# Scaling softmax rows in place and turning them with TensorE transposes, instead of matmuls with a diagonal of 1/sum

## The chip, the cores and the metric

The kernel runs on one core of a Trainium2 chip. The metric is the device time of one execution in microseconds (us), the median of several runs; lower is better. A core has a matrix engine (TensorE, PE in the profile, with its weight loads listed apart as PEld), a vector engine (VectorE, DVE), an activation engine (ScalarE, ACT), a general engine (GpSimd, POOL) and a queue engine that issues DMAs (SyncE, SP). Each engine works through its own queue in order. Matmuls write to PSUM, and only DVE and ACT read from there.

## The reference

Four transformer layers on 256 tokens of 1024 channels: neighbourhood attention with a context stream of another 256 tokens, sliding-window attention, a state space layer, and stick-breaking attention, each with a gated or squared-relu MLP. The change is in the softmax of the first two:

```python
s = jnp.concatenate([s_loc.reshape(B, H, GRID_W, n_loc), s_ctx], axis=-1)
p = jax.nn.softmax(s, axis=-1).astype(v.dtype)
p_loc = p[..., :n_loc].reshape(B, H, GRID_W, kh, kw)
p_ctx = p[..., n_loc:]
return (jnp.einsum('bhqkw,bkqwhd->bqhd', p_loc, v_win)
        + jnp.einsum('bhqc,bchd->bqhd', p_ctx, vc))
```

## The kernel before

Everything is float32. Products with weights are exact in three matmuls: weights and activations are split into a high and a low part (`split`, L228: ACT copies the high part, DVE subtracts), and `mm_w` and `mm_x` (L290 to L304) issue high by high, high by low and low by high. Weights come in by DMA parts of 512 KB or less as `raw`, and are split as `whi` and `wlo`.

The two attention stages work by chains. A chain is one head and one tile of 128 queries. In layer 0 there are 64: for each of 8 pairs of heads four chains over 512 keys (256 tokens and 256 of the context) and four context chains over 256 keys. In layer 1 there are 32, all over 512 keys. A chain runs through three functions:

- `score` (L1071, L1319): matmuls of q with k into a PSUM bank `sc`, a DVE addition of bias or mask, and `softmax_rows` (L818): DVE takes the row maximum (L821), ACT writes the exponentials to the tile `p` and their sum to `st` (L825), DVE takes the reciprocal of the sum (L829).
- `transposed` (L836): blocks of 128 columns of `p` are turned, so that keys lie on partitions, into a PSUM bank `pt`; then ACT and DVE, in turns, copy the bank to the SBUF tile `pT` (L843, L845).
- `finish` (L1087, L1330): for every second chain, matmuls of v with the two `pT` tiles into `po`, then a split to `oT`.

The turn and the scaling by 1/sum are one step before: `softmax_rows` makes `dg`, a diagonal matrix of 128 x 128 with each row's 1/sum (L831, `ts`, L122), and `transposed` multiplies each block by it:

```python
dg = at.tile([128, 128], F32, tag="dg", name="dg")
ts(dg, idn, st[:, 2:3], MUL)
T.matmul(pt[:, k * 128:(k + 1) * 128], lhsT=p[:, k * 128:(k + 1) * 128], rhs=dg)
```

In layer 0 the queries of the latent chains stand in reverse order within each row of 64 (the tile `q` is written reversed at L1017, since a bias table is read so), and `idn` is the constant `flip`, which turns them back; elsewhere it is the identity.

`run_chains` (L848) writes the chains in a staggered order: chain j is turned two chains (layer 1: three) after it was scored. Between chains stand pieces of other work (`fill`): the q and k products of the next pair of heads and their norms, in layer 1 the q products of the next group and the first part of the output product (`Early`, L319). The order in which instructions finally stand on each engine's queue is made by a scheduler from this program, with costs of its own for each instruction.

Of the kernel before, what the change touches and what calls it, by code (L numbers as in the profile page):

```python
# [24 lines left out]
def _layout():  # L25
    off = 0
    for name, n in (("id", 128), ("flip", 128), ("ones", 128), ("nam", 64), ("rc", 128),
                    ("rs", 128), ("sw0", 128), ("sw1", 128), ("hq", 2), ("dm", 16), ("eps", 1),
                    ("sel", 512)):
        _CL[name] = (off, off + n)  # L30
        off += n
    return off
# [5 lines left out]
def constants():  # L38
    c = np.zeros((128, _NC), np.float32)

    def put(name, a):
        s, e = _CL[name]
        c[:, s:e] = a

    p = np.arange(128)
    z = np.zeros((128, 128), np.float32)
    z[p, p] = 1.0
    put("id", z)
    f = np.zeros((128, 128), np.float32)
    f[p, (p // 64) * 64 + 63 - p % 64] = 1.0  # L50
    put("flip", f)
    put("ones", 1.0)
    col = 63 - p % 64
    start = np.clip(col - 8, 0, 48)
    kc = np.arange(64)
    ok = (kc[None] >= start[:, None]) & (kc[None] < start[:, None] + 16)
    put("nam", np.where(ok, 0.0, NEG).astype(np.float32))
    t = np.arange(256)
    inv = np.float32(10000.0) ** (-np.arange(16, dtype=np.float32) / np.float32(16))
    row = (t // 64).astype(np.float32)  # L60
    cl = (t % 64).astype(np.float32)
    ang = np.stack([row[:, None] * inv, cl[:, None] * inv], axis=1).astype(np.float32)
    cs, sn = np.cos(ang), np.sin(ang)
    cc = np.stack([cs, cs], axis=2).reshape(2, 128, 64)
    ss = np.stack([-sn, sn], axis=2).reshape(2, 128, 64)
    put("rc", cc.transpose(1, 0, 2).reshape(128, 128))
    put("rs", ss.transpose(1, 0, 2).reshape(128, 128))
    q, k = np.meshgrid(p, p, indexing="ij")
    put("sw0", np.where(k > q, NEG, 0.0))
    put("sw1", np.where(q > k, NEG, 0.0))  # L70
    put("hq", np.stack([np.where(p < 64, 0.125, 0.0), np.where(p < 64, 0.0, 0.125)], 1))
    put("dm", (p[:, None] % 16 == np.arange(16)[None]).astype(np.float32))
    put("eps", EPS)
    sel = np.zeros((128, 4, 128), np.float32)
    for q in range(4):
        sel[32 * q, q] = 1.0
    put("sel", sel.reshape(128, 512))
    return c
# [7 lines left out]
def _build(ctx, tc, I, out, dbg):  # L86
# [10 lines left out]
    last = [None]  # L97
# [51 lines left out]
    ident, flip, ones, eps = C("id"), C("flip"), C("ones"), C("eps")  # L149
# [22 lines left out]
    def vector_loads(va, cc):  # L172
        """loads of the small vectors, most urgent first."""
# [70 lines left out]
    class Weights:  # L244
        """src: dram view [128, kt, n] or [128, kt, n / 128, 128]; parts of at most 1024 elements."""
# [39 lines left out]
    def wpairs(w, s, c0):  # L285
        """two column tiles of 128, one in each of two neighbouring blocks of s columns."""
        b = w.rearrange("(k p) (b n) -> p k b n", p=128, n=s)
        return b[:, :, c0 // s:c0 // s + 2, c0 % s:c0 % s + 128]

    def mm_w(ps, w, c0, x, k, s0, s1, first, last_):  # L290
        """channel-major product, one contraction tile: weights stationary."""
# [6 lines left out]
    def mm_x(ps, w, c0, c1, x, k, t0, first, last_):  # L298
        """token-major product, one contraction tile: activations stationary."""
# [6 lines left out]
    def gemm_w(tiles, x, nk, s0, s1, evac, lead):  # L306
        """tiles: list of callables giving (weights, column, psum view, key); the first `lead` of them go
        through the contraction together, so that they can start before all of x is there."""
# [10 lines left out]
    class Early:  # L319
        """the first two column tiles of a product, begun while its last contraction tiles are still missing."""  # L320
# [78 lines left out]
    def square_sum(n, pooled, view=lambda v: v, late=KT - 2):  # L399
        """tiles whose columns sum, over the partitions, to those of h * h."""  # L400
# [20 lines left out]
    def rstd_rows(n, pooled=6, late=KT - 2):  # L421
        """1 / rms of every token, a quarter of them on each block of 32 partitions."""
# [19 lines left out]
    def rstd(n, pooled=6, late=KT - 2, tag="x"):  # L442
        """1 / rms of every token, on all partitions; left in PSUM."""
        return spread_cols(rstd_rows(n, pooled, late), n, tag)

    def rstd_cols(view=lambda v: v, pooled=6):
        """1 / rms of every token, tokens on partitions: [128, 2]; view gives the order of the tokens."""
# [11 lines left out]
    def gained(x, gain, view=lambda v: v):  # L459
        """x = gain * h, for products that are scaled by the tokens' 1 / rms afterwards."""  # L460
# [5 lines left out]
    def normed(x, r, n, gain, shift=None):  # L466
        """gain(k, v), shift(k, v): columns for contraction tile k and stream v."""
# [25 lines left out]
    def rsqrt(y, ss, n, pool):  # L493
        """y = 1 / sqrt(ss / 64 + eps), by a bit estimate and three Newton steps."""
# [10 lines left out]
    def head_scale(views, pool, scale=(None, None)):  # L505
        """1 / rms of every head of token-major products [128, 256] in PSUM, times a scale of the tokens."""
# [11 lines left out]
    def head_norm(views, pool, scale=(None, None)):  # L518
        """per-head normalisation of token-major products [128, 256]; views in PSUM."""
# [10 lines left out]
    def stack_q(o, q):  # L530
        """heads of q, token-major [128, n, 64], as blocks (high, low) of 128 columns."""
# [3 lines left out]
    def stack_k(oh, ol, k):  # L535
        """heads of k as blocks (high, high) and (low, low): with those of q, two products make the whole q k."""
# [12 lines left out]
    def cmul(o, a, b, t, conj=False, e=None):  # L549
        """o = a * b (pairs of real and imaginary views); conj: a * conj(b)."""  # L550
# [41 lines left out]
    class S5:  # L592
        """operators of the state space layer: e = a^s b, k = c a^t b, f = c a^t, and the phases of a^8t."""

        def __init__(self, pp, loads):
# [43 lines left out]
            # input matrix: ((a - 1) / lam) * b  # L639
# [32 lines left out]
        def c(self):  # L672
            pp, ct, ci, dr = self.pp, self.ct, self.ci, self.dr
            # output matrix, transposed: states onto partitions
# [101 lines left out]
        def phases(self, fp, hf):  # L776
            """powers 1..32 of exp(8 i theta), and |a|^8 with a zero where a new group starts."""
# [21 lines left out]
        def f(self, fp, i):  # L799
            """state-to-output matrices, a sixteenth of the groups: real(c a s) needs (re, -im) of c a."""  # L800
# [17 lines left out]
    def softmax_rows(ps, n, at, idn, tail=None):  # L818
        """rows of ps [128, n] -> unnormalised weights and idn scaled by the rows' 1/sum."""
# [10 lines left out]
        dg = at.tile([128, 128], F32, tag="dg", name="dg")  # L830
        ts(dg, idn, st[:, 2:3], MUL)  # L831
        return p, dg
# [3 lines left out]
    def transposed(p, dg, nk, at):  # L836
        pt = bank("pt")
        for k in range(nk):
            T.matmul(pt[:, k * 128:(k + 1) * 128], lhsT=p[:, k * 128:(k + 1) * 128], rhs=dg)
        pT = at.tile([128, 512], F32, tag="pT", name="pT", bufs=4)  # L840
        flip_evac[0] ^= 1
        if flip_evac[0]:
            act(pT[:, 0:nk * 128], pt[:, 0:nk * 128], AF.Copy)  # L843
        else:
            cp(pT[:, 0:nk * 128], pt[:, 0:nk * 128])  # L845
        return pT

    def run_chains(chains, lag):  # L848
        """chains: list of (score, probs, [finish of a group]); every group is two chains long.
        score() -> state, probs(state) -> transposed weights, finish([both])."""  # L850
# [13 lines left out]
    # ================ start ================  # L864
    w_pool("wsp", 4)
    with ExitStack() as sa:
# [92 lines left out]
        # ================ layer 0: mixer ================  # L959
# [4 lines left out]
        with ExitStack() as s0:  # L964
# [103 lines left out]
            def chain(pr, ctx_, qt, e, pre):  # L1068
                hd = 2 * pr + e

                def score():  # L1071
# [10 lines left out]
                    if ctx_:  # L1082
                        return softmax_rows(s_[:, 0:256], 256, at, ident)
                    tt(s_[:, 0:256], s_[:, 0:256], bts[hd, qt].rearrange("p r c -> p (r c)"), ADD)
                    return softmax_rows(s_, 512, at, flip)
# [15 lines left out]
                return (pre, score, lambda s_: transposed(*s_, 2 if ctx_ else 4, at), finish)  # L1101
# [33 lines left out]
        # ================ generic channel-major products ================  # L1135
        def w_tiles(src, ncols, ksteps=KT, r0=0, after=None):
            """column tiles of 128 of dram weights, loaded by chunks of at most 2048 elements."""
# [38 lines left out]
        with ExitStack() as s0:  # L1176
# [25 lines left out]
            # ================ layer 1: mixer ================  # L1202
# [4 lines left out]
        with ExitStack() as s0:  # L1207
# [4 lines left out]
            def rope(q, t, g):  # L1212
                """gain, then rotation of [128, 4 heads, 64] of tokens of tile t (None: gain alone)."""
# [58 lines left out]
            def q_steps(c, tag="g"):  # L1272
                """heads (8b + 2i, +1) of kv head 2b and the same four further on, of kv head 2b + 1"""
# [40 lines left out]
            def chain(c, s, qt, j, pre):  # L1314
# [4 lines left out]
                def score():  # L1319
# [8 lines left out]
                    return softmax_rows(s_, 512, at, ident, tail=sink[:, hd:hd + 1])  # L1328
# [12 lines left out]
                return (pre, score, lambda s_: transposed(*s_, 4, at), finish)  # L1341
# [41 lines left out]
    # ================ layer 1: the rest ================  # L1383
# [14 lines left out]
    def pair_products(src, n2, cols, x_, evac, lead, after=None):  # L1398
        """products with column tiles m and n2 + m of the weights, side by side."""
# [20 lines left out]
    # ================ S5 mixer ================  # L1420
    gT = [[actp.tile([128, 512], F32R, tag=f"o{p}{k}", name=f"g{p}{k}") for k in range(4)] for p in "hl"]
    gT = [[t[:, j * 256:(j + 1) * 256] for t in g_ for j in range(2)] for g_ in gT]
    with ExitStack() as s0:
# [4 lines left out]
        def spare_w():  # L1428
            """tiles of the pool of weight parts, which idles meanwhile."""
# [208 lines left out]
    # ================ stick-breaking attention ================  # L1638
# [146 lines left out]
    # ================ last gated mlp, and out ================  # L1785
# [44 lines left out]
```

## Time and profile before

| what | us |
|---|---|
| median of 3 runs | 1825.13 |
| lowest and highest run | 1824.33, 1829.41 |
| span of the profiled execution, first to last instruction | 1823.7 |
| PE busy in it | 1738.8 |
| DVE busy in it | 1183.4 |
| ACT busy in it | 790.0 |

The span leaves out what lies before the first and after the last instruction; of the profiled execution no other time is given, and its span is 1.4 us under the median of the runs. A PE busy time counts each matmul from its start to a modelled end; matmuls overlap in the array, so how long one holds the engine is read from starts that follow each other, not from its duration. A float32 matmul stands in the trace as two records, a float32 transpose as one.

### The profile page before, as it was taken

The page shows a single profiled execution, that of the slowest core. Times are in us where ns is not written, and L with a number is a line of the kernel's source. Part 1 is how long each engine was busy: PE and PEld are TensorE (multiplying, and loading weights), DVE is VectorE, ACT ScalarE, POOL GpSimd, SP SyncE. Part 2 cuts the span into 40 slices and gives each one's busy share as a digit, 9 for nine tenths or more (in the row PEclk, how much of TensorE's full clock was granted, in tenths as well). Part 3 has the DMA queues.
Part 4 walks back from the last instruction along what each step waited for, and adds up shares of the span by engine and source line. Part 5 has one row for each costly group of instructions (what it writes and reads, how often), then busy time and mean ns, then how long its engine had stood idle before and what let it go on. Part 6 is the DMA issues. An engine that isn't in the chain of part 4 may idle for free. (4 is left out here: it accounts for less than half of the span.)

```text
span 1823.7 us, 34377 instructions
## 1 busy us (share of the span) xinstructions
PE 1738.8 (95%) x13449; PEld 1537.9 (84%) x13449; DVE 1183.4 (65%) x2508; ACT 790.0 (43%) x1446; POOL 473.1 (26%) x633
## 2 busy tenths in 40 slices
PE   5899999999999999999999999998999999999999
PEld 3478888877777777888878999987899999889998
DVE  8556776775635434346986656768576788958674
ACT  4344444442413222223654545545444465535453
POOL 5311211115789300030102000202331332324130
PEclk8899999999999999999999999998999999999999
DMA  8565454325566655332215566688558564435852
GB/s 221 172 175 155 147 173 122 106 86 162 170 212 219 184 170 162 93 93 81 59 36 146 155 189 186 193 303 235 142 153 231 152 218 131 127 93 167 228 156 88
DMA packets 441045, 286.68 MB, mean 157 GB/s; under 512 B 50450, under 2 KB 418610, under 8 KB 440882
## 3 DMA queue, kind: packets, MB, share of 16 engines
q1 hardware_dynamic: 439122, 278.70, 52.4%
q0 software_dynamic: 1760, 5.77, 0.8%
q8 instruction: 106, 1.74, 0.4%
q14 instruction: 57, 0.47, 0.1%
HBM read 271.48 MB, written 17.15 MB: 158 GB/s over the span
## 5 line engine op out<-in xcount | busy, mean ns | idle before, releaser
L111 ACT ACTIVATE whi<-raw 128x1024 fp32r<-128x1024 f32 (+2 forms) x388 | 389.8, 1013 | 482.2 <-PE g L295 352.3
L114 DVE TENSOR_TENSOR wlo<-raw,whi 128x1024 fp32r<-128x1024 f32 (+2 forms) x388 | 466.4, 1207 | 189.8 <-ACT whi L111 186.7
L296 PE MATMUL g<-xh,wlo 128*128 128x256 f32 (+1 forms) x1216 | 375.2, 309 | 5.5 <-DVE wlo L114 5.2
L294 PE MATMUL g<-xh,whi 128*128 128x256 f32 (+1 forms) x1216 | 375.2, 310 | 1.3 <-ACT xh L111 1.2
L295 PE MATMUL g<-xl,whi 128*128 128x256 f32 (+1 forms) x1216 | 374.6, 308 | 0.0
L294 PE MATMUL g<-oh,whi 128*128 128x256 f32 (+1 forms) x1056 | 332.1, 315 | 3.3 <-DVE hc L117 1.4
L296 PE MATMUL g<-oh,wlo 128*128 128x256 f32 (+1 forms) x1056 | 331.0, 314 | 0.0
L295 PE MATMUL g<-ol,whi 128*128 128x256 f32 (+1 forms) x1056 | 330.8, 313 | 0.0
L296 PEld LDWEIGHTS g<-xh,wlo 128*128 128x128 f32 x1216 | 235.2, 193 | 17.9 <-DVE wlo L114 7.4
L294 PEld LDWEIGHTS g<-xh,whi 128*128 128x128 f32 x1216 | 234.7, 193 | 16.4 <-ACT whi L111 3.1
L295 PEld LDWEIGHTS g<-xl,whi 128*128 128x128 f32 x1216 | 235.3, 193 | 9.7
L294 PEld LDWEIGHTS g<-oh,whi 128*128 128x128 f32 x1056 | 198.3, 188 | 23.6 <-issue 3.9
L295 PEld LDWEIGHTS g<-ol,whi 128*128 128x128 f32 x1056 | 198.3, 188 | 15.3 <-issue 1.1
L296 PEld LDWEIGHTS g<-oh,wlo 128*128 128x128 f32 x1056 | 198.3, 188 | 14.5 <-issue 0.2
L302 PE MATMUL g<-whi,xh 128*128 128x256 f32 x560 | 166.9, 298 | 3.8 <-ACT xh L111 2.8
L303 PE MATMUL g<-wlo,xh 128*128 128x256 f32 x560 | 161.1, 288 | 0.6 <-DVE wlo L114 0.6
L304 PE MATMUL g<-whi,xl 128*128 128x256 f32 x560 | 160.5, 288 | 0.1
L117 DVE SCALAR_TENSOR_TENSOR h<-g,mods,h 128x256 f32<-128x256 f32 x64 | 30.8, 482 | 141.5 <-PE g L296 141.5
L302 PEld LDWEIGHTS g<-whi,xh 128*128 128x128 f32 x560 | 108.6, 194 | 13.3 <-issue 8.5
L303 PEld LDWEIGHTS g<-wlo,xh 128*128 128x128 f32 x560 | 108.8, 194 | 2.2 <-DVE wlo L114 1.7
L304 PEld LDWEIGHTS g<-whi,xl 128*128 128x128 f32 x560 | 108.1, 194 | 0.5 <-DVE xl L117 0.3
L111 ACT ACTIVATE oh<-t 128x256 fp32r<-128x256 f32 (+1 forms) x108 | 51.3, 482 | 125.5 <-DVE t L114 125.5
(300 smaller groups left out, 2943.3 us busy)
## 6 DMA issues: line engine op xcount, KB each, us to landing
raw<-mlp_w SPq DMA_DIRECT2D x128, 512.0 KB, 4.6
ada<-ada_w SPq DMA_DIRECT2D x88, 512.0 KB, 5.4
raw<-ffn_w_up SPq DMA_DIRECT2D x88, 512.0 KB, 5.2
raw<-ffn_w_down SPq DMA_DIRECT2D x32, 384.0 KB, 3.6
raw<-ffn_w_down SPq DMA_DIRECT2D x32, 320.0 KB
raw<-na_wqkv SPq DMA_DIRECT2D x32, 256.0 KB, 4.4
raw<-a_w_glu SPq DMA_DIRECT2D x16, 512.0 KB, 7.9
raw<-w_kv SPq DMA_DIRECT2D x16, 512.0 KB, 4.5
```

Of the source, the lines that this page charges most:

```text
L111: last[0] = A.activation(out=o, in_=i, func=f, **kw)
L114: (e or V).tensor_tensor(out=o, in0=a, in1=b, op=op)
L117: V.scalar_tensor_tensor(out=o, in0=a, scalar=s, in1=b, op0=op0, op1=op1)
L294: T.matmul(ps, lhsT=a, rhs=xh[k][:, s0:s1], start=first, stop=False)
L295: T.matmul(ps, lhsT=a, rhs=xl[k][:, s0:s1], start=False, stop=False)
L296: T.matmul(ps, lhsT=b, rhs=xh[k][:, s0:s1], start=False, stop=last_)
L302: T.matmul(ps, lhsT=xh[k][:, t0:t0 + 128], rhs=a, start=first, stop=False)
L303: T.matmul(ps, lhsT=xh[k][:, t0:t0 + 128], rhs=b, start=False, stop=False)
L304: T.matmul(ps, lhsT=xl[k][:, t0:t0 + 128], rhs=a, start=False, stop=last_)
```

## The change

`softmax_rows` no longer makes `dg`. It scales the whole tile `p` by 1/sum in place on DVE, 512 or 256 columns of 128 partitions. `transposed` turns the blocks with TensorE transposes, whose other operand is the constant identity. For the latent chains of layer 0 the queries are turned back by the copy from PSUM to `pT`, which reads each 64 columns in reverse. The constant `flip` is gone, so the tile of constants is 1363 columns wide instead of 1491. The other lines of the diff are comments taken out, so that line numbers from L17 to L830 stand 1 to 3 lower in the changed kernel; they are left out here.

```diff
-    def softmax_rows(ps, n, at, idn, tail=None):
+    def softmax_rows(ps, n, at, tail=None):
...
         V.reciprocal(out=st[:, 2:3], in_=st[:, 1:2])
-        dg = at.tile([128, 128], F32, tag="dg", name="dg")
-        ts(dg, idn, st[:, 2:3], MUL)
-        return p, dg
+        ts(p[:, 0:n], p[:, 0:n], st[:, 2:3], MUL)
+        return p
...
-    def transposed(p, dg, nk, at):
+    def transposed(p, nk, at, turned=False):
         pt = bank("pt")
         for k in range(nk):
-            T.matmul(pt[:, k * 128:(k + 1) * 128], lhsT=p[:, k * 128:(k + 1) * 128], rhs=dg)
+            T.transpose(pt[:, k * 128:(k + 1) * 128], p[:, k * 128:(k + 1) * 128], ident)
         pT = at.tile([128, 512], F32, tag="pT", name="pT", bufs=4)
+        o, i = pT[:, 0:nk * 128], pt[:, 0:nk * 128]
+        if turned:
+            o, i = o.rearrange("p (a x) -> p a x", x=64), i.rearrange("p (a x) -> p a x", x=64)[:, :, 63::-1]
         flip_evac[0] ^= 1
         if flip_evac[0]:
-            act(pT[:, 0:nk * 128], pt[:, 0:nk * 128], AF.Copy)
+            act(o, i, AF.Copy)
         else:
-            cp(pT[:, 0:nk * 128], pt[:, 0:nk * 128])
+            cp(o, i)
         return pT
...
-                        return softmax_rows(s_[:, 0:256], 256, at, ident)
+                        return softmax_rows(s_[:, 0:256], 256, at)
                     tt(s_[:, 0:256], s_[:, 0:256], bts[hd, qt].rearrange("p r c -> p (r c)"), ADD)
-                    return softmax_rows(s_, 512, at, flip)
+                    return softmax_rows(s_, 512, at)
...
-                return (pre, score, lambda s_: transposed(*s_, 2 if ctx_ else 4, at), finish)
+                return (pre, score, lambda s_: transposed(s_, 2 if ctx_ else 4, at, not ctx_), finish)
...
-                    return softmax_rows(s_, 512, at, ident, tail=sink[:, hd:hd + 1])
+                    return softmax_rows(s_, 512, at, tail=sink[:, hd:hd + 1])
...
-                return (pre, score, lambda s_: transposed(*s_, 4, at), finish)
+                return (pre, score, lambda s_: transposed(s_, 4, at), finish)
```

The number of instructions in the queues is the same on every engine. Their order differs in the two attention stages and nowhere else. Two places:

DVE in layer 0, around the second latent chain's scale. Ahead of it stand the norm of the next heads (`rq`, `ri`, `rt`, the steps of a reciprocal square root) and the third chain's bias, row maximum and copy. Before:

```order
L114 TENSOR_TENSOR sc<-sc,bt 128x256
L117 SCALAR_TENSOR_TENSOR rt<-rt,rq 128x8
L821 TENSOR_REDUCE st<-sc 128x1
L117 SCALAR_TENSOR_TENSOR ri<-rt,ri 128x8
L127 COPY pT<-pt 128x512
L114 TENSOR_TENSOR rt<-ri 128x8
L829 RECIPROCAL st<-st 128x1
L117 SCALAR_TENSOR_TENSOR rt<-rt,rq 128x8
L122 TENSOR_SCALAR dg<-cst,st 128x128
```

With the change:

```order
L124 COPY pT<-pt 128x512
L114 SCALAR_TENSOR_TENSOR rt<-rt,rq 128x8
L818 TENSOR_REDUCE st<-sc 128x1
L114 SCALAR_TENSOR_TENSOR ri<-rt,ri 128x8
L111 TENSOR_TENSOR rt<-ri 128x8
L114 SCALAR_TENSOR_TENSOR rt<-rt,rq 128x8
L114 SCALAR_TENSOR_TENSOR ri<-rt,ri 128x8
L111 TENSOR_TENSOR rt<-ri 128x8
L114 SCALAR_TENSOR_TENSOR rt<-rt,rq 128x8
L826 RECIPROCAL st<-st 128x1
L114 SCALAR_TENSOR_TENSOR ri<-rt,ri 128x8
L119 TENSOR_SCALAR p<-p,st 128x512
```

The copy of the turned block now stands ahead of the row maximum, and the reciprocal and the scale stand four small norm steps later.

PE in layer 1. Before, from the matmuls of v ahead of the 12th chain's turn: behind the turn come products with weights for the next group of q (`g<-whi,xh` and its two partners).

```order
L1324 MATMUL sc<-ka_8505,qz_9226 128x512
L1334 MATMUL po<-pT,vv 64x128 x7
L839 MATMUL pt<-dg,p 128x128 x4
L1324 MATMUL sc<-kb_8507,qz_9226 128x512
L1334 MATMUL po<-pT,vv 64x128
L303 MATMUL g<-wlo,xh_8350 128x256
L304 MATMUL g<-whi,xl_8358 128x256
L302 MATMUL g<-whi,xh_8351 128x256
L303 MATMUL g<-wlo,xh_8351 128x256
L304 MATMUL g<-whi,xl_8359 128x256
```

With the change, from the 16th chain's turn to the 18th's:

```order
L1334 MATMUL po<-pT,vv 64x128
L836 MATMUL pt<-cst,p 128x128 x4
L1324 MATMUL sc<-ka_8442,qz_9470 128x512
L1324 MATMUL sc<-kb_8444,qz_9470 128x512
L1334 MATMUL po<-pT,vv 64x128 x7
L1324 MATMUL sc<-ka_8442,qz_9477 128x512
L1324 MATMUL sc<-kb_8444,qz_9477 128x512
L836 MATMUL pt<-cst,p 128x128 x4
L1324 MATMUL sc<-ka_8442,qz_9477 128x512
L836 MATMUL pt<-cst,p 128x128 x4
L1324 MATMUL sc<-kb_8444,qz_9477 128x512
```

The products for q now all stand ahead of the 8th chain's turn, before the change ahead of the 13th's; from the 8th turn to the 20th PE has next to nothing but the chains.

## Rows read from the trace of the kernel before

**Rows 1.** The page: the span, and each engine's busy time and instructions.
```profile
span 1823.7 us, 34377 instructions
PE 1738.8 (95%) x13449; PEld 1537.9 (84%) x13449; DVE 1183.4 (65%) x2508; ACT 790.0 (43%) x1446; POOL 473.1 (26%) x633
```

**Rows 2.** Stretches of both chains: busy us of PE, PEld, DVE, ACT, POOL, clock.
```profile
132.00:406.00 274.00, 270.40 (x2370) 235.70 (x2370) 194.62 (x627) 121.38 (x308) 49.02 (x59) 0.99 0.45 132
880.00:985.00 105.00, 99.65 (x805) 84.25 (x805) 88.08 (x326) 57.32 (x148) 2.41 (x3) 0.98 0.15 44
```

**Rows 3.** Waits of PE on another engine, layer 0 chains, then layer 1 chains.
```profile
PE pt L839 <- DVE dg L122: 0.6, 1, 0.6
...
PE pt L1300 <- DVE pT L127: 2.5, 2, 1.6
```

**Rows 4.** Records of two lines of PE: durations in ns, minimum, median, maximum.
```profile
L839 PE MATMUL pt<-dg,p x640: 270/275/583, 132.7 to 978.3; 128*128 128x128 f32 x160
L1742 PE MATMUL pt<-cst,be x48: 271/273/329, 1526.2 to 1600.1; 128*128 128x128 f32 x48
```

**Rows 5.** Timeline of PE (start, us busy): diagonal matmuls, later float32 transposes.
```profile
303.28 1.16 PE L839 MATMUL pt<-dg,p 128*128 128x128 f32 x8
304.19 0.36 PE L302 MATMUL g<-whi,xh 128*128 128x256 f32 x1
...
1526.16 0.49 PE L1742 MATMUL pt<-cst,be 128*128 128x128 f32 x3
1526.49 0.72 PE L1675 MATMUL pt<-cst,qn 128*128 128x128 f32 x4
1526.97 0.36 PE L302 MATMUL g<-whi,xh 128*128 128x256 f32 x1
```

**Rows 6.** Groups of DVE by line and shape: count, busy us, mean ns.
```profile
L122 DVE TENSOR_SCALAR dg<-cst,st 128x128 f32<-128x128 f32 x96 | 27.4, 286 | 1.1
L114 DVE TENSOR_TENSOR h<-g,h 128x256 f32<-128x256 f32 x40 | 16.2, 420 | 19.3 <-PE g L296 19.3
L117 DVE SCALAR_TENSOR_TENSOR h<-g,mods,h 128x256 f32<-128x256 f32 x64 | 30.8, 482 | 141.5 <-PE g L296 141.5
L114 DVE TENSOR_TENSOR ol<-po,oh 128x512 fp32r<-128x512 f32 x8 | 5.5, 684 | 1.8 <-ACT oh L111 1.8
L122 DVE TENSOR_SCALAR qz<-pt,vt 128x512 f32<-128x512 f32 x4 | 3.0, 739 | 0.0
L127 DVE CAST q<-pt 128x512 fp32r<-128x512 f32 x8 | 5.4, 676 | 0.8 <-PE pt L1013 0.8
```

**Rows 7.** Layer 0 in 10 us windows: first and last of six, of 28.
```profile
152.00:162.00 10.00, 9.78 (x95) 8.36 (x91) 9.62 (x27) 6.07 (x14) 3.16 (x3) 1.00 0.66 181
372.00:382.00 10.00, 10.00 (x80) 8.67 (x79) 9.25 (x33) 5.03 (x14) 0.78 (x2) 1.00 0.63 182
```

**Rows 8.** Layer 1 in four windows, columns as in rows 2.
```profile
880.00:896.00 16.00, 16.00 (x127) 15.19 (x126) 15.68 (x55) 11.13 (x24) 0.00 (x0) 1.00 0.34 99
896.00:925.00 29.00, 29.00 (x239) 24.51 (x238) 24.90 (x102) 15.95 (x44) 0.00 (x0) 1.00 0.07 20
925.00:951.00 26.00, 22.28 (x191) 18.30 (x191) 24.00 (x97) 14.47 (x40) 0.00 (x0) 0.99 0.07 21
951.00:978.00 27.00, 27.00 (x215) 21.85 (x212) 19.42 (x69) 13.37 (x39) 0.00 (x0) 0.94 0.14 40
```

**Rows 9.** Windows around a fall of the granted clock, then of the last attention.
```profile
947.25:950.66 3.41, 1.80 (x18) 1.32 (x18) 3.41 (x13) 1.58 (x5) 0.00 (x0) 1.00 0.00 0
950.66:954.07 3.41, 3.41 (x18) 2.53 (x16) 2.65 (x6) 0.74 (x2) 0.00 (x0) 0.50 0.00 0
1584.00:1598.00 14.00, 12.14 (x76) 7.81 (x74) 13.77 (x22) 7.58 (x19) 11.33 (x34) 1.00 0.27 76
```

**Rows 10.** Transposes of PE within two of these windows, by line.
```profile
L1300 PE MATMUL pt<-idr,sq 128*128 128x128 f32 x8 | 1.2, 253 | 1.6 <-DVE pT L127 1.6
...
L1742 PE MATMUL pt<-cst,be 128*128 128x128 f32 x18 | 3.2, 285 | 1.3 <-DVE be L114 0.9 <-DVE pT L127 0.4
```

More of the change, by code (lines that the diff above doesn't have):

```diff
@@ L26, in _layout @@
     off = 0
-    for name, n in (("id", 128), ("flip", 128), ("ones", 128), ("nam", 64), ("rc", 128),
+    for name, n in (("id", 128), ("ones", 128), ("nam", 64), ("rc", 128),
                     ("rs", 128), ("sw0", 128), ("sw1", 128), ("hq", 2), ("dm", 16), ("eps", 1),
@@ L48, in constants @@
     put("id", z)
-    f = np.zeros((128, 128), np.float32)
-    f[p, (p // 64) * 64 + 63 - p % 64] = 1.0
-    put("flip", f)
     put("ones", 1.0)
@@ L147, in C @@
         return cst[:, s:e]
-    ident, flip, ones, eps = C("id"), C("flip"), C("ones"), C("eps")
+    ident, ones, eps = C("id"), C("ones"), C("eps")
     vt = const.tile([128, 384], F32, name="vt")
```

## Prediction

> **What bounds the kernel now.** I read the page first [rows 1]: PE is busy 95% of the span, DVE 65%. An average over a whole program says little about one stage, so next come the two stretches that the change touches [rows 2]. In layer 0 PE is busy 270.4 of 274 us and DVE 194.6 (71%); in layer 1 PE 99.7 of 105 and DVE 88.1 (84%). Then the waits of PE inside the chains [rows 3]: 0.6 us in all for the diagonal in layer 0, 2.5 us for copied blocks in layer 1. So PE hardly waits, and what is taken off its queue shortens a stage until DVE has no room left. How near that point is shows only in short windows. In layer 0, of 28 windows of 10 us from 132 us on, six have DVE busy for 9.0 us or more; the first and the last of them stand in [rows 7]. In layer 1 I cut at the changes of pattern [rows 8]: in 880 to 896 both engines are full (DVE 15.68 of 16), in 896 to 925 PE is full and DVE at 24.90 of 29, in 925 to 951 DVE (24.00 of 26) leaves PE idle for 3.7 us, and in 951 to 978 PE is full and DVE at 19.42 of 27.
>
> **PE: what is removed.** There are 64 chains in layer 0, half with four blocks and half with two, so 192 blocks, and 32 chains with four in layer 1, so 128: 320 in all. Before, a block is two records: 640 for 320 [rows 4]. A float32 transpose elsewhere in this kernel (L1742) is one: 48 records for 16 chains with three each. Durations (275 and 271 ns) say nothing, since records overlap; the starts do [rows 5]. Four blocks by the diagonal hold PE from 303.28 to 304.19, 0.91 us or 0.228 a block. Three transposes go from 1526.16 to 1526.49, four from 1526.49 to 1526.97: 0.11 to 0.12 each. I take 0.11 us saved per block: 21.1 us in layer 0, 14.1 in layer 1, 35.2 in all. The low end is 0; the trace excludes that transposes hold PE longer than now, at this clock.
>
> **DVE: what is added.** `dg` (128 columns) costs 0.286 us, 96 times [rows 6]. The scale has 512 columns in 64 chains and 256 in 32. No row has exactly this operation from SBUF in place. Two float32 tensors cost 420 ns at 256 columns and 684 at 512, so 1.03 ns a column; a scalar read per partition adds some 62 ns (482 against 420). An operation at that slope with 128 columns would take 420 - 132 + 62 = 350 ns, yet `dg` takes 286. So an operation on one SBUF tensor runs below that slope; near half of it (0.53 ns) is my reading. Then 512 columns cost 286 + 384 x 0.53 = 489 ns, and 256 cost 354. Bounds: no less than `dg` itself, 286; no more than the pointer scale from PSUM, 739 ns at 512 (`qz`), and 482 at 256. I take 489 and 354, since `dg` is the nearest row: the same operation, SBUF to SBUF, same operands. DVE gains 32 x 0.203 + 32 x 0.068 = 8.7 us in layer 0 and 32 x 0.203 = 6.5 in layer 1; at the high end 20.8 and 14.5.
>
> The Trainium skill's page "VectorE: DVE Perf Modes", section "The perf-mode tier table", says that a float32 tensor_scalar on SBUF goes at twice the pace of a tensor_tensor, and that an operand in PSUM takes this away. By its figure for 2,048 columns (1,227 ns), an estimate for 512 is some 0.43 us, and the whole sum below would come to about 1805. The trace agrees as far as `dg` reaches; no row has the wide scale.
>
> **Waits and moved steps.** The turn now waits for the scale instead of the diagonal, 0.2 us later after the same reciprocal, and in the order shown for DVE four small norm steps stand ahead of it as well. What is queued behind it on PE are the scores and v products of other chains. The cover is that a chain is turned two chains (layer 0, some 4.3 us each) or three (layer 1, some 3.1 us each) after its score, so some 8 to 9 us; that PE waited 0.6 us for `dg` in layer 0 [rows 3] says that the cover holds. I take nothing; if the cover were gone, the whole scale would be exposed (a rival below). The reversed read from PSUM: the reversed write of `q` from PSUM takes 676 ns at 512 columns, a forward addition 684 [rows 6], so nothing on DVE. For ACT no row shows it; ACT is busy 121 of 274 us in layer 0 [rows 2], and at twice the price of today for half of the 32 copies it would still have room. The scheduler moves 33 issues on SP and 6 on POOL within the two stages; weights for the next products are then asked for somewhat earlier or later, while the DMA share is 0.45 in layer 0 and 0.15 in layer 1, so nothing again. The constants are 64 KB smaller: nothing.
>
> **The sum.** Layer 0: in 22 of 28 windows PE sets the pace and its saving counts, 21.1 x 22/28 = -16.6. In the six where DVE is full the saving is lost and DVE's extra counts, 8.7 x 6/28 = +1.9. Together -14.7. Layer 1, by [rows 8]: 880 to 896, three chains on a full DVE, +0.6. In 896 to 925, nine chains, PE needs 29 - 36 x 0.11 = 25.0 and DVE 24.90 + 9 x 0.203 = 26.7; DVE is never packed perfectly, so I take some way between 26.7 and 29, -1.5. In 925 to 951, eight chains on DVE, +1.6. In 951 to 978, twelve chains, PE needs 21.7 and DVE 21.9: 5.1 to gain, taken as -4. Together -3.3. DVE is busy for 84.0 of these 98 us, so 90.4 with the scale: layer 1 cannot gain more than 7.6 us whatever PE saves. Total -18.0. The profiled span is 1823.7, 1.4 us under the median of the runs; I carry that over: 1825.1 - 18.0 = **1807 us**.
>
> **Rivals.** *Full saving.* The new order spreads DVE's work so that PE's 35.2 us count in full: 1790. For it: a scheduler may fill DVE's slack, 79 us in layer 0. Against it: the bound of 7.6 us in layer 1 allows only 21.1 + 7.6 = 28.7, or 1796; for the rest PE would have to save more per block than read.
>
> *The scale at its high price.* In place, with input and output the same tile, the scale might lose the fast pace and cost 0.74 us. Layer 0: -16.6 + 20.8 x 6/28 = -12.1. Layer 1: +1.4, 0 (DVE 29.0 of 29), +3.6 and some -1.5, so +3.5. Total -8.6: 1816.5. `dg` speaks against it, no row for a wide tile excludes it.
>
> *No change.* DVE's high price stands exposed on every chain, 35.3 us against 35.2 saved: 1825. This wants DVE to set the pace everywhere, which 79 us of slack in layer 0 speak against.
>
> *Slower: the clock.* PE gets half speed in some stretches. After 947.25 to 950.66, in which PE is busy for 1.80 of 3.41 us, the granted clock stands at 0.50 for the next 3.41 us, the lower of two levels (1.2 instead of 2.4 GHz) [rows 9]. Eight of the 18 matmuls ahead of that fall are transposes [rows 10]. If attention with transposes, and with more idle time of PE between them, drew this fall again and again, each such 3.41 us would cost up to 1.7. To be slower by over 5.5 us it must first eat the 18 gained: 23.5 / 1.7, or some 14 stretches of half clock. In all 28 that fit into the 95 us of layer 1 it would be +48, less 18: 1855. Against it: from 1584 to 1598 PE is busy 12.14 of 14 us with 18 transposes of L1742 among 76 matmuls, at a clock of 1.00 [rows 9, 10], and in 925 to 951 PE already idles 3.7 us and loses little of its clock. I take one such stretch more or less as inside the range.
>
> The Trainium skill's page "TensorE: Matmul & The Clock Gate", section "Part 4: PE-mode transpose", says that the full clock does not engage for transposes, as these do not count as PE work in the same way. By that rule alone the result would be this rival's 1855 at the most. The trace speaks against it where transposes stand among other matmuls, as they do here, and does not exclude it at 947 to 954.
>
> *It does not do what it says* (a float32 transpose as two passes, like the product): excluded by the 48 records of L1742 [rows 4].
>
> **How the numbers follow.** The forecast, 1798 to 1814 on its own, has 0.62; the full saving (1788 to 1797) 0.13; the high price (1814 to 1821) 0.12; no change 0.08; the clock 0.05. The range of 1789 to 1820 takes in the first three but for their edges and leaves out the last two. About 0.3%, 5.5 us, is what a measurement of this kernel can tell from no change. Faster by more than that, below 1819.7: the forecast and the full saving, and most of the high price, 0.85. Within 0.3%: no change and the edge of the high price, 0.10. Slower: 0.05.
>
> **What would show it.** In the profile of the changed kernel the turn must be 320 records with starts 0.11 to 0.12 us apart; 640 or 0.2 would take the forecast's ground away. The scale's group shows 0.49 or 0.74 us for 512 columns, and with it which case it is. The stage that was 132 to 406 us should end some 15 us earlier, the one from 880 on be some 3 us shorter, with DVE over 90% busy there and waits of PE for a scaled `p` or a copied `pT` where DVE is full. Layer 0 gaining far less than 15 us with DVE idle would mean that the cover of the turn is gone: then the transposes' group shows idle time ahead of it, put down to DVE's scale. A granted clock of 0.50 in several windows of layer 1 would show the last rival. A changed time in any stage outside these two would be nothing that I reasoned about.

## The result and the profile after

The changed kernel takes 1812.5 us (median of 4 runs, 1810.9 to 1814.1), the kernel before 1827.3 (4 runs, 1824.3 to 1829.7, one more than the forecast started from): a ratio of 0.991, 95% interval 0.990 to 0.993, so 14.8 us faster. The profiled execution has a span of 1809.2 us against 1823.7, 14.5 us less; all that follows is read from it. The page of the changed kernel, its span and engines [rows 1]:

```profile
span 1809.2 us, 33749 instructions
PE 1717.4 (95%) x13129; PEld 1504.4 (83%) x13129; DVE 1197.0 (66%) x2508; ACT 790.6 (44%) x1446; POOL 470.6 (26%) x633
```

PE has 320 matmul records fewer, DVE 13.6 us more work. To place the 14.5 us I cut both traces at the same instructions: layer 0 from the first turn of q (`turn`, L1013) to the last product with v, layer 1 from the first score to the last product with v. The columns are busy us (instructions) of PE, PEld, DVE, ACT, POOL, then the mean granted clock, the DMA share and GB/s. Before:

```profile
115.97:405.59 289.62, 282.70 (x2472) 246.73 (x2473) 200.98 (x644) 128.00 (x322) 52.72 (x64) 0.99 0.47 135
886.81:980.20 93.39, 89.25 (x722) 74.55 (x721) 77.92 (x305) 51.34 (x138) 0.00 (x0) 0.98 0.12 34
```

The changed kernel:

```profile
116.71:392.13 275.42, 269.57 (x2281) 226.06 (x2281) 207.07 (x644) 127.23 (x322) 54.48 (x64) 0.99 0.49 141
873.00:967.50 94.50, 81.82 (x594) 61.24 (x593) 83.12 (x305) 52.41 (x138) 0.00 (x0) 0.91 0.12 34
```

Layer 0 is 14.2 us shorter. Layer 1 is 1.1 us longer, although PE is busy for 7.4 us less there. What lies ahead of layer 0 (+0.7), between (-0.4) and behind (-1.7) is code that the change doesn't touch; in the kernels below those three parts move by up to three us too, once by 4.5, so a difference of that size in one profile means nothing there.

The scale as groups of DVE, over the whole span, then at 512 columns in layer 0 and in layer 1 alone:

```profile
L119 DVE TENSOR_SCALAR p<-p,st 128x512 f32<-128x512 f32 x64 | 32.2, 504 | 0.5
L119 DVE TENSOR_SCALAR p<-p,st 128x256 f32<-128x256 f32 x32 | 12.2, 383 | 0.3
...
L119 DVE TENSOR_SCALAR p<-p,st 128x512 f32<-128x512 f32 x32 | 16.9, 530 | 0.5
...
L119 DVE TENSOR_SCALAR p<-p,st 128x512 f32<-128x512 f32 x32 | 15.2, 478 | 0.0
```

The turn, as starts on PE (start, us busy; the first row of each pair is a turn, the second what follows it):

```profile
226.38 0.66 PE L836 MATMUL pt<-cst,p 128*128 128x128 f32 x4
226.79 0.36 PE L299 MATMUL g<-whi,xh 128*128 128x256 f32 x1
...
233.75 0.44 PE L836 MATMUL pt<-cst,p 128*128 128x128 f32 x2
233.94 0.36 PE L299 MATMUL g<-whi,xh 128*128 128x256 f32 x1
```

The scale costs 0.504 us at 512 columns in the mean (0.489 was forecast) and 0.383 at 256 (0.354). The means are drawn up by a few in layer 0: 61 of the 64 wide ones take 0.470 to 0.490 us, all of layer 1's among them, and the other three 0.98 to 1.02, each beside a running GpSimd instruction; at 256 columns most take 0.342 to 0.355 us, and the two longest, 0.82 and 0.91, also run beside GpSimd. In layer 1, where GpSimd is idle, the mean is 0.478. Four transposes hold PE for 0.41 us and two for 0.19, about 0.10 a block, where four products by the diagonal held it for 0.91 [rows 5]. That is 0.125 us saved a block; over all 192 blocks of layer 0, from the start of each turn to the start of what follows, 44.5 us became 22.7, or 0.114 a block. The forecast was 0.11.

In layer 1 the granted clock falls twice. For each fall, the 3.4 us ahead of it and the time at half clock:

```profile
907.30:910.72 3.42, 1.41 (x6) 0.59 (x4) 3.42 (x14) 1.15 (x5) 0.00 (x0) 1.00 0.00 0
910.72:920.96 10.24, 7.89 (x37) 5.84 (x38) 8.10 (x28) 4.99 (x14) 0.00 (x0) 0.50 0.00 1
931.30:934.70 3.40, 1.57 (x8) 0.69 (x5) 3.40 (x15) 1.72 (x6) 0.00 (x0) 0.99 0.00 0
934.70:941.53 6.83, 4.50 (x27) 3.71 (x28) 5.96 (x19) 2.67 (x7) 0.00 (x0) 0.51 0.00 0
```

Ahead of each fall DVE is busy without a gap and PE for less than half of the time. Then PE runs at 0.50, 17.1 us in all, or five stretches of 3.41 us; before it was one [rows 9]. What PE waits for, by the waits of that stage, is the next group's q, whose norm and rotation stand on DVE between the chains' steps (us in total, times, longest; before, the same wait was 0.6 us, once, beside the 2.5 of [rows 3], which are 0.9 now):

```profile
PE pt L1300 <- DVE sq L111: 5.4, 2, 2.7
```

### The profile page after: what moved, and what is told of

Same layout as the page of the kernel before. It is cut to its first block, busy times and chain, and to the rows that moved or that the text cites. A ratio compares the mean times of both kernels' runs of the same rounds, so it can differ in the third digit from the quotient of the medians.

```text
span 1809.2 us, 33749 instructions
## 1 busy us (share of the span) xinstructions
PE 1717.4 (95%) x13129; PEld 1504.4 (83%) x13129; DVE 1197.0 (66%) x2508; ACT 790.6 (44%) x1446; POOL 470.6 (26%) x633
## 5 line engine op out<-in xcount | busy, mean ns | idle before, releaser
L293 PEld LDWEIGHTS g<-oh,wlo 128*128 128x128 f32 x1056 | 198.4, 188 | 14.5 <-issue 0.3
```

The costliest lines, as they stand in the source:

```text
L293: T.matmul(ps, lhsT=b, rhs=xh[k][:, s0:s1], start=False, stop=last_)
```

## The experiments

Three theories for layer 1. **A**: DVE's time for the scale is what it pays. **B**: layer 1 gains, and something else falls short. **C**: the new order of the steps costs it. A fourth price, the half clock, is told apart on the way. Stages are cut as above, each in the one profiled execution of its kernel; the half clock is counted in layer 1, in stretches of 3.41 us, the length of the fall in [rows 9]. Each ratio is to runs of the kernel before taken beside that kernel (medians 1827.3 to 1829.7).

Two limits hold for all of it. The changed kernel and e1, e4, e6, e7, e8, e14 and e15 have the same layer 0 in the same order, and it took 274.4 to 276.2 us: a stage from one profile is good to about 1 us. And the scheduler orders the queues anew for each program. In layer 1 only before and e1, e4 and e11, and e6 and e9 share an order on PE and DVE, so every other comparison there changes the order along with the work.

| kernel | median, us | ratio to before | layer 0 | layer 1 | half clock |
|---|---|---|---|---|---|
| before | 1827.3 | | 289.6 | 93.4 | 1 |
| changed | 1812.5 | 0.990 to 0.993 | 275.4 | 94.5 | 5 |
| e1, layer 0 only | 1810.1 | 0.988 to 0.992 | 275.4 | 93.3 | 1 |
| e2, no scale | 1796.6 | 0.981 to 0.985 | 265.1 | 82.8 | 1 |
| e3, identity by matmul | 1839.4 | 1.004 to 1.008 | 291.2 | 100.1 | 2 |
| e4, layer 1 copies on ACT | 1807.2 | 0.987 to 0.990 | 276.2 | 88.6 | 4 |
| e6, layer 1 scale on GpSimd | 1815.3 | 0.990 to 0.995 | 275.4 | 95.3 | 1 |
| e7, filler | 1814.2 | 0.989 to 0.995 | 275.3 | 95.8 | 1 |
| e8, held order | 1820.5 | 0.994 to 0.997 | 275.1 | 103.2 | 7.7 |
| e9, both scales on GpSimd | 1823.8 | 0.995 to 0.998 | 280.9 | 99.3 | 4 |
| e11, all copies on ACT | 1800.1 | 0.982 to 0.987 | 269.3 | 87.6 | 3 |
| e14, lag of four | 1807.5 | 0.986 to 0.990 | 274.4 | 91.1 | 4 |
| e15, GpSimd and lag of four | 1810.6 | 0.988 to 0.992 | 275.9 | 93.0 | 4 |
| e16, e11 and lag of four | 1799.8 | 0.981 to 0.985 | 270.2 | 85.9 | 4 |

**One layer alone (e1).** Layer 1 keeps the diagonal:

```diff
+        if diag:
+            dg = at.tile([128, 128], F32, tag="dg", name="dg")
+            ts(dg, ident, st[:, 2:3], MUL)
+            return p, dg
```

> Layer 0 as changed, layer 1 as before (diagonal of 1/sum and matmuls). Theory A, DVE fills in layer 1 and PE, starved, falls to half clock, so the change gains nothing there: the time is that of the changed kernel, 1812 within 3 us, and the granted clock of 0.50 in the chains of layer 1 shrinks from five stretches of 3.41 us to one or two. Rival B, layer 1 does gain what its PE saving says and layer 0 falls short: 1815 to 1818, above the changed kernel.

1810.1 us, not to be told from the changed kernel by their intervals, and layer 1 back at 93.3 us with one stretch at half clock. The profiled execution was its slowest, 1814.8 us; what it has over the others is not in the two stages. The whole gain is layer 0's; B is out.

**One part of the change each (e2, e3).** e2 leaves out the scale, and with it the division by the row sums; e3 keeps it and turns by a product with the identity:

```diff
-        ts(p[:, 0:n], p[:, 0:n], st[:, 2:3], MUL)
```

> The changed kernel without the scale; the division by the row sums is left out. DVE is 64 x 0.48 + 32 x 0.35 = 42 us less busy than in the changed kernel, 27 less than before. Theory A, the work on DVE is what ate layer 1's gain: layer 1 falls 7 to 10 us below before, layer 0 some 19 to 21 below; in all 1796 to 1800, at full clock in layer 1 but for one stretch. Rival C, the order in which the steps now stand (the products for q all ahead of the chains) is what costs layer 1, and not the scale's work: layer 1 as in the changed kernel, 1808 to 1812, with the falls of the clock.

```diff
-            T.transpose(pt[:, k * 128:(k + 1) * 128], p[:, k * 128:(k + 1) * 128], ident)
+            T.matmul(pt[:, k * 128:(k + 1) * 128], lhsT=p[:, k * 128:(k + 1) * 128], rhs=ident)
```

> The scale stays, but the turn is a matmul with the identity in two passes: PE's load as before, DVE's as changed. Theory A: layer 0 loses all its gain and 1 to 3 us more, since DVE is full in few windows; layer 1 is slower than before by 3 to 6 us; in all 1829 to 1834. If DVE's extra is hidden wherever PE is the slower engine: 1827 within 1.5. If it is the thinner load of PE that drops the clock and costs layer 1 its gain, layer 1 here has no more half clock than before, and is no slower than in the changed kernel.

Both stages of e2:

```profile
117.64:382.72 265.08, 260.34 (x2280) 222.92 (x2281) 185.88 (x580) 127.75 (x322) 54.33 (x64) 0.99 0.51 147
865.37:948.15 82.78, 75.01 (x594) 57.62 (x593) 71.97 (x273) 50.98 (x138) 0.00 (x0) 0.98 0.14 39
```

and of e3:

```profile
116.36:407.56 291.20, 285.82 (x2472) 246.97 (x2473) 208.85 (x644) 128.57 (x322) 53.21 (x64) 0.99 0.47 134
893.25:993.35 100.10, 92.42 (x721) 77.03 (x721) 83.87 (x305) 52.34 (x138) 0.00 (x0) 0.97 0.11 33
```

Together with before and the changed kernel these make steps. From before to e3 the scale takes the diagonal's place (and the reversed copy that of `flip`), while PE's products stay two records a block: layer 0 +1.6 us for 7.9 us more on DVE, layer 1 +6.7 for 6.0 more, one more stretch at half clock among it. From e3 to the changed kernel the turn changes: layer 0 -15.8, layer 1 -5.6, with three more stretches at half clock. So on this path the scale is nearly hidden in layer 0 and most of PE's saving counts; in layer 1 the scale comes out at its full price, and PE's saving at less than half of the 14.1 us of the forecast. Without the scale the stages fall by another 10.3 and 11.7 us, 21.2 and 11.2 us of DVE's time. They stand 24.5 and 10.6 us below before, more than theory A asked for (19 to 21, and 7 to 10). So once PE's products are shorter, half of the scale's time is paid in layer 0 too. Where PE gets it back there is not shown: its listed waits in layer 0 sum to 5.4 us in the changed kernel and 3.8 in e2.

e3 also answers the third case of its expectation. With PE's old load, layer 1 has a stretch more at half clock than before and is 5.6 us slower than in the changed kernel: a thinner load of PE is not what costs layer 1 its gain. e2, with the thin load and one stretch, says the same.

e3 came out 5 us above its expectation. The excess is not in the two stages (+8.3 in sum, 4 to 9 expected) but between them, in code that is the same: 481.2 us before, 485.7 in e3. Right behind layer 0, up to 500 us, before and then e3:

```profile
405.59:500.00 94.41, 89.15 (x463) 67.97 (x461) 53.34 (x83) 35.09 (x55) 59.25 (x100) 1.00 0.51 167
```

```profile
407.56:500.00 92.44, 86.72 (x423) 65.57 (x421) 51.09 (x79) 31.81 (x50) 58.30 (x100) 0.94 0.50 159
```

A clock of 0.94 there is three stretches, some 10 us, at half speed. Between the same instructions e3 falls back by 3.4 us while they last, and by 0.9 more at one longer wait for DVE (`adacc`). That is a warning for every number here that is smaller than 5 us and rests on whole times.

**Work off DVE (e4, e11).** The copies of turned blocks, shared by ACT and DVE, go to ACT alone, in layer 1 and then in both layers (e11's edit; e4 does the same by an argument that only layer 1 sets):

```diff
-        flip_evac[0] ^= 1
-        if flip_evac[0]:
-            act(o, i, AF.Copy)
-        else:
-            cp(o, i)
+        act(o, i, AF.Copy)
```

> The changed kernel with all 32 copies of turned blocks of layer 1 on ACT, where 16 were on DVE: DVE 16 x 0.68 = 10.9 us less, ACT 16 x 0.60 = 9.6 more, of 58 busy in 107. Theory A: layer 1 shortens by 5 to 9 us and the falls of the clock become fewer: 1803 to 1808. Rival C (order): no change, 1811 to 1814. If ACT becomes the one that is waited for (its exponentials late by the copies): slower than the changed kernel.

> The changed kernel with all copies of turned blocks on ACT, in both layers: in layer 0 a further 17.7 us off DVE (207 of 275 us busy), some 16 onto ACT (127 of 275). If DVE's time still limits layer 0 as the kernel without a scale says (that took 21 us off DVE and 10.3 off the stage): layer 0 falls from 275.4 to 268 to 271, layer 1 as in the run with its copies on ACT (88.6), in all 1800 to 1803. If what the scale costs in layer 0 is the wait for it and not DVE's time: layer 0 at 275 or above, 1806 to 1809.

e4 takes 9.4 us off DVE in layer 1 (83.1 to 73.7) and the stage falls by 5.9, as A says; the clock was to fall less often, and does so by one stretch only, four instead of five. e11 takes 11.7 us off DVE in layer 0 and the stage falls by 6.1, half of it. ACT does the same copy in less time than DVE: 595 ns (e11) against 686 (changed kernel, layer 0), the reversed read among them. Layer 1 of e4, then of e11, and the two copies:

```profile
874.38:962.93 88.55, 78.71 (x593) 61.08 (x593) 73.70 (x289) 60.33 (x154) 0.00 (x0) 0.92 0.13 36
868.45:956.03 87.58, 77.48 (x594) 60.44 (x593) 73.67 (x289) 60.28 (x154) 0.00 (x0) 0.94 0.13 37
```

```profile
L108 ACT ACTIVATE pT<-pt 128x512 f32<-128x512 f32 x64 | 37.9, 595 | 47.6 <-PE pt L836 47.2
```

```profile
L124 DVE COPY pT<-pt 128x512 f32<-128x512 f32 x16 | 11.0, 686 | 4.4 <-PE pt L836 4.2
```

**The scale on another engine (e6, e9, e15).** `ts(..., e=G)` in layer 1, in both layers, and in layer 1 with a longer lag:

> The changed kernel with the scale of layer 1 on GpSimd, which stands idle there: DVE 32 x 0.48 = 15.4 us less, on GpSimd about 1 to 1.9 us each (its 128 x 256 operations take 0.56 to 1.0). Theory A (DVE's time for the scale is what layer 1 pays): the chains of layer 1 fall from 94.5 us to near the 82.8 of the kernel without a scale, in all 1800 to 1805. Rival, the waiting for the scale is what costs (a chain longer by 1 to 2 us): layer 1 stays at 94 or above, 1812 or more.

> The changed kernel with the scale of both layers on GpSimd. DVE 42 us less than in the changed kernel. If DVE is what limits the gain in both stages and GpSimd keeps up: near the kernel without a scale, 1797 to 1802. If GpSimd's own work in layer 0 (54 of 275 us, the biases ahead of the scores) delays scores: layer 0 above the 275 us of the changed kernel, 1805 or more in all.

The layer 1 stage of e6, then of e9, whose layer 1 is the same code in the same order on PE:

```profile
874.13:969.46 95.33, 78.92 (x594) 58.94 (x593) 75.25 (x273) 52.03 (x138) 51.88 (x32) 0.98 0.12 34
```

```profile
882.08:981.34 99.26, 82.98 (x594) 61.87 (x593) 75.22 (x273) 51.96 (x138) 51.91 (x32) 0.93 0.12 32
```

DVE is busy for 7.9 us less than in the changed kernel, and nothing is gained: A's 1800 to 1805 fell, the rival held. GpSimd takes 1.56 us (median) for 512 columns, where DVE takes 0.50, and PE stood and waited for it:

```profile
PE pt L836 <- POOL p L119: 10.5, 16, 1.2
```

So not DVE's time alone is paid, but the time from the row's sum to the turn, with DVE's queue in it. In layer 0 e9 loses 5.4 us, the size of its second case, but by 8.4 us in which PE waits for GpSimd's scale and not by late scores. The test of A is not clean, though: without the scale DVE is busy for 71.97 us in layer 1 (e2), in e6 for 75.25. Eleven of its other instructions take over 0.15 us longer than their like in e2 (`t<-qn,cst` 0.83 us for 0.42), and each of them runs beside a GpSimd scale.

Two pairs with the same code and order give the price of the clock. e4 and e11 are 0.97 us apart in layer 1, with one stretch more at half clock in e4. e6 and e9 are 3.9 us apart, with three more in e9; but 0.9 of it is there within the first six us, before the clock falls in either, where an exponential on ACT comes late. That leaves 3.0, or 1.0 us for one. Whole runs agree: of sixteen of the kernel before, taken beside e6 to e9, the three at a mean granted clock of 0.980 took 1826.6 us in the mean, the three at 0.976 took 1831.0. A line through all sixteen falls by 1.27 us for each 0.001 of the clock, lines through the seven beside each of three other groups of kernels by 0.8 to 1.1; 0.001 of 1825 us is 3.65 us at half speed, so 0.7 to 1.2 us for 3.41.

> The scale of layer 1 on GpSimd as before (1.56 us each; PE waited 10.5 us for it), with four chains of lag. If that wait was all that kept the freed DVE time from counting: the stage falls from 95.3 us to 83 to 89, in all 1801 to 1808. If not: 93 to 97, 1812 to 1816.

With four chains of lag the wait for GpSimd shrinks to 6.1 us and the stage to 93.0, at a mean clock of 0.93, and the time, 1810.6 us, falls between the two cases. The wait was part of it, not "all that kept the freed DVE time from counting".

```profile
PE pt L836 <- POOL p L119: 6.1, 10, 0.9
```

**The clock (e7).** Twelve matmuls without use ahead of each turn of q:

```diff
+                        for _ in range(6):
+                            T.matmul(pq.bitcast(F32), lhsT=idr, rhs=kst["a", 0][:, 0, :], start=True, stop=True)
```

> The changed kernel with 12 idle 512-column matmuls of TensorE ahead of each of the three turns of q inside the chains of layer 1, some 0.24 us each, 2.9 us per turn, into a bank that the turn overwrites; nothing else is altered. If the half clock is what costs layer 1 its gain: fewer half-clock stretches, and the stage shorter than 94.5 us by up to 4 in spite of the 8.6 us of added work. If the half clock falls only into time in which PE waits for DVE anyway: clock restored or not, the stage is 94.5 or up to 8 longer.

One stretch at half clock is left, and the stage takes 95.8 us, 1.3 more than in the changed kernel for some 8.6 us of added work (twelve start within 2.88 us, 886.60 to 889.48). It also holds 27 products with weights, some 3.2 us by their starts, that the changed kernel does ahead of its first score. So the second case of the expectation holds.

```profile
886.60 3.04 PE L1299 MATMUL pt<-ka,idr 128*128 128x512 f32 x12
889.48 0.40 PE L1326 MATMUL sc<-kb,qz 128*128 128x512 f32 x1
```

The filler buys the clock back and eats what it gave. It does not say what a restored clock alone would give; that wasn't tried.

**The order (e8).** The products that stand between the chains are tied on PE behind the preceding turn:

```diff
+                                with tc.issue_after(turn_ins[0].ins):
+                                    f()
```

> The changed kernel with the products for q (and the first products of the output) in layer 1 held on PE's queue behind the turn of the chain that precedes them in the program, so that they are spread over the chains and not drawn ahead of them. Rival C (the order costs layer 1 its gain): the stage falls from 94.5 us to 86 to 90, without the falls of the clock; in all 1804 to 1808. Theory A (DVE's work): the stage stays within 2 us of 94.5, whatever stands between the chains on PE.

103.2 us, 8.7 more, with nearly eight stretches at half clock and 14.7 us of PE waiting for q. Here too 27 products moved into the stage; counted from the end of layer 0 the two kernels are 8.4 us apart. C is out in the form in which I put it: drawing the products ahead is better than spreading them this way. It doesn't show that no better order exists, and since the other kernels have orders of their own, what the order does in each of them is not shown.

**More time in the chain (e14, e16).** Each chain of layer 1 is turned four chains after its score, with five tiles `p` instead of three and seven `st` instead of four; no work is added:

```diff
-            run_chains(chains, 3)
+            run_chains(chains, 4)
```

> The changed kernel with each chain of layer 1 turned four chains after its score and not three, with five tiles p and seven st for it: more time between the scale and the turn that waits for it, no work added or taken away. If layer 1 pays for the scale as a longer wait in the chain: 94.5 us fall to 86 to 91, in all 1804 to 1809. If it pays DVE's time, the engine being full when PE starves: 93 to 96, 1811 to 1814.

> All copies of turned blocks on ACT in both layers, and four chains of lag in layer 1. If the two add up, DVE's time and the wait being separate prices: layer 0 as with the copies alone (269.3), layer 1 from 87.6 to 83 to 86, in all 1795 to 1799. If the lag only helps where DVE is the full engine: layer 1 stays at 87 to 89, 1799 to 1802.

e14 takes 3.4 us off layer 1 (91.1, at the edge of the 86 to 91 that the wait was to give), at 83.15 us of DVE, as in the changed kernel (83.12). More lag and more tiles come together here; which of them does it was not tried:

```profile
870.94:962.07 91.13, 78.04 (x593) 60.80 (x593) 83.15 (x305) 52.55 (x138) 0.00 (x0) 0.93 0.12 35
```

e16's layer 1 is 85.9 us, 1.7 less than e11's, as if the two prices added up in part, but its time, 1799.8, is e11's within the intervals, as the other case has it. In all of these PE goes on waiting for q: 5.4 us in the changed kernel, 7.3 in e14, 6.6 in e16. No run moved that. In e16:

```profile
PE pt L1296 <- DVE sq L111: 6.6, 4, 3.1
```

## Why the prediction held, and which term did not

1. *The time.* Forecast 1807, 18.0 us less than before; measured 1812.5, 14.8 less, inside the range of 1789 to 1820 and inside the forecast's own 1798 to 1814.
2. *PE's saving.* One record for a block instead of two: 320 for 640. The 0.11 us for a block measured 0.114 over layer 0 (0.125 in the one turn shown).
3. *The scale.* Forecast 0.489 and 0.354 us, measured 0.470 to 0.490 and mostly 0.342 to 0.355 where GpSimd was not running beside it, 0.504 and 0.383 in the mean: the value by the half slope, not the high price of 0.739. In place it keeps the fast pace. That a scale beside GpSimd can take twice as long stood in no term; it came out for five of 96. The estimate from the Trainium skill's "VectorE: DVE Perf Modes", section "The perf-mode tier table", 0.43 us at 512 columns, was lower than what the rows show.
4. *Layer 0.* -14.7 forecast, -14.2 measured. Its two parts come out alone in e3: the extra on DVE was to cost 1.9 us and cost 1.6; the saving on PE was to bring 16.6 and brought 15.8. Counting windows in which DVE is full was a good price on that path. It is not one for DVE's time in the changed kernel: there e2 gets back 10.3 us for 21.2 and e11 6.1 for 11.7, half and not 6/28. How the -14.2 divides thus depends on which part is changed first, and that both parts came so close is in part luck; 1.6 us is also little above what one profile can tell. The cover of the turn held: the waits of PE in that stage list none of the turn.
5. *Layer 1.* -3.3 forecast, +1.1 measured. This is the term that was mis-sized, by 4.4 us. "I take one such stretch more or less as inside the range" was too few: the half clock came in four stretches more, at about 1 us each some 4 us. Worked out, not shown by a run: at the clock of before the stage would be about 94.5 - 4 = 90.5, near the 90.1 of the forecast. What starved PE there was sized too small as well. The scale was counted only where DVE stood full already (+0.6, +1.6) or netted against PE's saving, but e3 has +6.7 for it. The two overlap, since the falls follow PE's waits for DVE, and can't be added; no run divides the 4.4 us between them and the new order. The signs came out in part: DVE is busy for 88% of the stage, not over 90%, and PE waits 2.7 us for copied blocks but 5.4 for the next q, a wait that the prediction did not name, and for no scaled `p`.
6. *The clock rival.* The mechanism appeared, at a smaller size than the rival needed (14 stretches) and at a lower price (about 1 us for the "up to 1.7"). It isn't the transposes that draw it: the kernel without a scale has the same 320 transposes and one stretch, and e8, with them too, nearly eight. What stands ahead of each fall shown is PE waiting for DVE. The Trainium skill's "TensorE: Matmul & The Clock Gate", "Part 4: PE-mode transpose", lets expect no full clock for transposes; here turns among other matmuls run at a granted clock of 1.00 (from 222 to 232 us, where the first turn shown stands; 0.99 over layer 0).
7. *DVE as the bound in layer 1.* Right in direction, too simple as a mechanism. Work off DVE gives time back (e2, e4), but work moved to a slower engine does not (e6), and more lag with more tiles does some (e14). What PE waits for is a chain of steps through DVE's queue, and both the work in the queue and the length of the chain count. How the 6.7 us divide between them, and what the order has in it, stays open.

## What to carry to other kernels

Price a trade between two engines stage by stage: the same trade gave 14 us where one engine had slack, and nothing where both were nearly full. The receiving engine was 69% busy in the one stage before, 83% in the other. Where it is that full, count all of what is added to it and ask what the other will do while it waits; here PE lost its clock. Then look for work on the receiving engine that a third one can do as fast: moving the copies to ACT turned the change's 0.991 into 0.985, while moving both scales to GpSimd, three times slower at it, gave most of the gain back (0.997).

## What had not been expected of the hardware

- A half-clock stretch of 3.41 us costs about 1 us of time in this kernel, not the 1.7 that a busy PE at half speed would lose: 0.97 and 1.0 by two pairs of profiles with the same code and order, 0.7 to 1.2 by lines through runs of one kernel.
- Code that is not touched can run at another clock: e3 lost 3.4 us between the two layers in three stretches that the kernel before does not have there.
- A scale on DVE beside a running GpSimd instruction took up to twice its time (0.98 to 1.02 us for 0.48, three of 64), and in layer 1 of e6 eleven of DVE's other instructions took longer beside GpSimd's scale than in e2 without it.
- ACT copies 512 columns from PSUM in 595 ns, reversed or not, DVE in 686.
- GpSimd scales 128 x 512 in place in 1.56 us (median), DVE in 0.50.
